# Four products a group moved behind the next group's eight, and one small load moved to another queue

## The chip, the cores and the metric

The kernel runs on one core of one Trainium2 chip. The metric is the device time of one execution in microseconds (us). Three executions of the kernel before took 1425.3, 1425.72 and 1429.72 us; the median is 1425.72 us.

## What is computed

One layer of a hybrid encoder on an input x of 256 rows by 2048 columns, in float32:

```python
h = rms_norm(x, norm_g)
u = h @ w_in                                    # 2048 x 22672
y_a, y_b, y_c, y_d = conv(u), rwkv7(u), forgetting_attention(u), pooling(u)   # 256 x 1024 each
merged = sum(sigmoid(logits_n(u) + b_merge[n]) * (y_n @ w_branch[n]) for n in range(4))
out = rms_norm(x + merged @ w_out, final_g)
```

Nearly all arithmetic is in three families of matrix products: with w_in (2048 x 22672), with the four w_branch (1024 x 2048) and with w_out (2048 x 2048). The weights are streamed from HBM once.

## The kernel before

**Chunks and groups.** A chunk is up to 512 columns of a weight matrix. It is computed for both 128-row blocks b = 0 and 1 of the 256 rows, each in its own PSUM bank (`psm`). The sum over the 2048 (or 1024) inputs goes in steps k of 128, and KG = 2 steps make a group g, so a chunk has 8 groups (4 for w_branch). There are 65 chunks: 45 of w_in, 16 of w_branch and 4 of w_out.

**Exact products from halves.** A float32 weight tile is split into a high part `wh` (a rounded copy) and a low part `wl` (the remainder); the activations are kept split in the same way (`xh` and `xl`, later `yah` and so on). Per step k and block b three products are added up in one bank: high activation by high weight (line 246), high activation by low weight (line 247), low activation by high weight (line 248). A group thus has 2 blocks x 2 steps x 3 = 12 products, each 128 x 128 by 128 x 512.

**The path of a group's weights.** SyncE (SP) loads a group's `raw` tile (line 265, 3 buffers). ScalarE (ACT) copies each of its two steps to `wh` (line 273; 6 buffers, that is three groups). VectorE (DVE) subtracts to get `wl` (line 274, 6 buffers). TensorE (PE) then runs the products. A `raw` buffer comes free when VectorE has made its `wl`; `wh` and `wl` buffers come free when the last product that reads them is done.

**Banks.** The pool of `psm` has three banks and a chunk takes two, in rotation. The first bank of a new chunk has long been empty; the second is the one that held block 0 of the chunk just ended, so the block 1 products of the new chunk wait until that one has been read out (by ScalarE at lines 290, 296, 304, 665 and so on, or by VectorE at lines 722, 734, 778, 860, 862, 899).

**Order.** Every engine has a list of instructions that it works off in order. A planner writes the lists ahead of time (line 951): of the instructions that are ready by its own timeline it takes the one with the best priority. Loads and splits of weights have the best priority (WEIGHTS), then the RWKV and attention chains, then everything else, the products among them, in the order of the program. ScalarE and VectorE also do all of the RWKV, attention, convolution and pooling work, mostly in the first 800 us; the products fill TensorE around it.

**The start.** `head(0)` loads the identity (line 173), then x_quarter(0) loads the first half quarter of x (line 207), the first step of the first weights (line 324), `norm_g` as `ng16` (line 326), the second half quarter and the second step, all on SP's queue. `norm_g` is transposed on TensorE (line 213), copied to `ngT` (line 214), and scales every `xh` and `xl` tile (lines 224, 225).

**The end.** The last w_out chunk (`keep`) computes block 0 group by group, keeping all split weights, and then block 1 from the kept ones.

Of the kernel before, what the change touches and what calls it, by code (L numbers as in the profile page):

```python
# [17 lines left out]
P = 128  # L18
T = 256
NB = 2  # L20
# [4 lines left out]
KG = 2  # L25
# [69 lines left out]
def kernel(  # L95
# [27 lines left out]
    nc = tc.nc  # L123
# [28 lines left out]
    @contextmanager  # L152
    def level(n):
        own, tc.cur_priority = tc.cur_priority, at[n]
        yield
        at[n], tc.cur_priority = tc.cur_priority, own
# [15 lines left out]
    def load_constants(lo, hi):  # L172
        nc.sync.dma_start(out=cst[:, lo:hi], in_=consts[:, lo:hi])
# [26 lines left out]
    ng16 = xin.tile([16, P], F32, name="ng16")  # L200

    def x_quarter(q):

        xt = xin.tile([P, NB, CH], F32, name=f"x{q}")
        for s in (range(2) if q == 0 else ()):
            cols = slice(s * CH // 2, (s + 1) * CH // 2)
            nc.sync.dma_start(out=xt[:, :, cols], in_=x_v[:, :, cols])
            first_weights(s)
        if q:
            nc.sync.dma_start(out=xt, in_=x_v[:, :, q * CH:(q + 1) * CH])  # L210
        if q == 0:
            tp = psum_ex("c")
            nc.tensor.transpose(tp[:, 0:16], ng16, ident[:16, :16])
            v.tensor_copy(out=ngT, in_=tp[:, 0:16])
        for k2 in range(2):
            tp = psum_ex("c" if k2 else "r")
            for j in range(2):
                for b in range(NB):
                    c0 = (2 * k2 + j) * P
                    nc.tensor.transpose(tp[:, j * T + b * P:j * T + (b + 1) * P], xt[:, b, c0:c0 + P], ident)  # L220
            for j in range(2):
                k = q * 4 + k2 * 2 + j
                s = tp[:, j * T:(j + 1) * T]
                last = sc.activation(out=xh[:, k, :], in_=s, func=AF.Copy, scale=ngT[:, k:k + 1])
                v.scalar_tensor_tensor(out=xl[:, k, :], in0=s, scalar=ngT[:, k:k + 1],
                                       in1=xh[:, k, :].bitcast(F32), op0=ALU.mult, op1=ALU.subtract)
        return xt, last
# [11 lines left out]
        v.tensor_scalar(out=nrstd8, in0=rstd, scalar1=-float(H) ** -0.5, scalar2=None, op0=ALU.mult)  # L239


    def products(ps, sth, stl, wh, wl, k, nk, n, b):
        cols = slice(b * P, (b + 1) * P)
        o = ps[b][:, :n]
        h, l = wh[:, :n], wl[:, :n]
        nc.tensor.matmul(o, lhsT=sth[:, k, cols], rhs=h, start=k == 0, stop=False)  # L246
        nc.tensor.matmul(o, lhsT=sth[:, k, cols], rhs=l, start=False, stop=False)  # L247
        nc.tensor.matmul(o, lhsT=stl[:, k, cols], rhs=h, start=False, stop=k == nk - 1)  # L248

    def new_ps():  # L250
        return [ps_main.tile([P, CH], F32, name="psm", tag="psm") for b in range(NB)]

    def chunk(ranges, nk, sth, stl, before=lambda g: None, keep=None):


        ps = new_ps()
        n = sum(r[2] for r in ranges)
        for g in range(nk // KG):
            wh, wl = [], []
            with level(WEIGHTS):  # L260
                raw = before(g)
                at = 0
                for wv, c0, w in ranges if raw is None else ():
                    raw = raw or wpool.tile([P, KG, CH], F32, name="raw", bufs=3)
                    nc.sync.dma_start(out=raw[:, :, at:at + w], in_=wv[:, g * KG:(g + 1) * KG, c0:c0 + w])
                    at += w
                for j in range(KG):
                    if keep:
                        h, l = keep(g * KG + j)
                    else:  # L270
                        h = wpool.tile([P, CH], F32R, name="wh", bufs=6)
                        l = wpool.tile([P, CH], F32R, name="wl", bufs=6)
                    sc.activation(out=h[:, :n], in_=raw[:, j, :n], func=AF.Copy)  # L273
                    v.tensor_tensor(out=l[:, :n], in0=raw[:, j, :n], in1=h[:, :n].bitcast(F32), op=ALU.subtract)  # L274
                    wh.append(h)
                    wl.append(l)
            for b in range(1 if keep else NB):
                for j in range(KG):
                    products(ps, sth, stl, wh[j], wl[j], g * KG + j, nk, n, b)
        if keep:  # L280
            for k in range(nk):
                products(ps, sth, stl, *keep(k), k, nk, n, 1)
        return ps

    def chunk_in(c0, n=CH, before=lambda g: None):
        return chunk([(w_in_v, c0, n)], D // P, xh, xl, before)
# [33 lines left out]
    def first_weights(j):  # L320

        if j == 0:
            first_raw.append(wpool.tile([P, KG, CH], F32, name="raw", bufs=3))
        nc.sync.dma_start(out=first_raw[0][:, j, :], in_=w_in_v[:, j, O_B + HALF:O_B + 2 * HALF])
        if j == 0:
            nc.sync.dma_start(out=ng16, in_=norm_g[0].rearrange("(k p) -> k p", p=P))

    def head(g):
        if g == 0:
            load_constants(0, P)  # L330
        if g == 6:
            load_constants(P, N_CONST)
        if g in (0, 1, 3, 5):
            xq.append(x_quarter(len(xq)))
        return first_raw[0] if g == 0 else None

    ps_first = chunk_in(O_B + HALF, before=head)
    with tc.issue_after(xq[3][1].ins):
        for q in range(4):
# [399 lines left out]
    def b_inputs(hf):  # L739
        t = [rw.tile([P, NB, HALF], F32, name="u" + nm) for nm in "rkv"]  # L740
        c0 = O_B + hf * HALF
        for j in range(3):
            if j == 2 and hf == 1:

                n0 = 328
                ps = chunk_in(c0 + 2 * W, n0)
                for b in range(NB):
                    sc.activation(out=t[2][:, b, 0:n0], in_=ps[b][:, 0:n0], func=AF.Copy, scale=rstd[:, b:b + 1])
                n1 = HALF - n0
                lu = wk.tile([P, NB, P], F32, name="qk", bufs=2)  # L750
                cf = wk.tile([P, NB, 16], F32, name="cf")
                ps = chunk([(w_in_v, c0 + 2 * W + n0, n1 + P), (w_in_v, O_CF, 16)], D // P, xh, xl)
                for b in range(NB):
                    for dst, lo, hi in ((t[2][:, b, n0:HALF], 0, n1), (lu[:, b, :], n1, n1 + P),
                                        (cf[:, b, :], n1 + P, n1 + P + 16)):
                        sc.activation(out=dst, in_=ps[b][:, lo:hi], func=AF.Copy, scale=rstd[:, b:b + 1])
                lora_and_forget(lu, cf)
            else:
                evac(t[j], ps_first if j == 0 and hf == 1 else chunk_in(c0 + j * W))
        return t  # L760
# [60 lines left out]
    for hf in range(2):  # L821
# [4 lines left out]
        for g2 in range(2):  # L826
            g = hf * 2 + g2
# [12 lines left out]
            for b in range(NB):  # L840
                for j in range(2):
                    nc.tensor.matmul(tp[:, b * T:(b + 1) * T], lhsT=pT[:, j, b * P:(b + 1) * P], rhs=pw[:, j, :],
                                     start=(j == 0), stop=(j == 1))
# [9 lines left out]
    for dc in range(4):  # L853
        mg = wk.tile([P, NB, CH], F32, name="va")
        for n, nm in enumerate("abcd"):
            gt = gate_tile(dc, n)
            ps = chunk([(w_br_v[n], dc * CH, CH)], W // P, *yT[nm])
            for b in range(NB):
                if n == 0:
                    v.tensor_tensor(out=mg[:, b, :], in0=ps[b], in1=gt[:, b, :], op=ALU.mult)  # L860
                else:
                    v.tensor_tensor(out=gt[:, b, :], in0=ps[b], in1=gt[:, b, :], op=ALU.mult)
                    v.tensor_tensor(out=mg[:, b, :], in0=mg[:, b, :], in1=gt[:, b, :], op=ALU.add)
        split_T([mh[dc // 2], ml[dc // 2]], (dc % 2) * 4, mg, 4)
# [18 lines left out]
    def keep(k):  # L883
        if k < 8:
            return spare[0][:, k, :], spare[1][:, k, :]
        i = 2 + 2 * ((k - 8) // 4)
        return spare[i][:, k % 4, :], spare[i + 1][:, k % 4, :]

    for dc in range(4):
        fg = bcast(final_g[dc * CH:(dc + 1) * CH])  # L890
        ps = chunk([(w_out_v, dc * CH, CH)], D // P, Parts(mh), Parts(ml), keep=keep if dc == 3 else None)
        cs = slice((dc % 2) * CH, (dc % 2 + 1) * CH)
        last = dc == 3
        n = CH // 2 if last else CH
# [60 lines left out]
```

## Time and profile before

| | |
|---|---|
| median of three executions | 1425.72 us |
| the profiled execution | 1430.22 us |
| its span, first to last instruction | 1428.4 us |
| PE busy | 1390.6 us (97%), 6961 matmuls and as many weight loads |
| DVE busy | 983.7 us (69%) |
| ACT busy | 743.1 us (52%) |
| HBM read | 257.44 MB |
| granted TensorE clock, mean | 0.995 |

Busy time of PE is modelled: matmuls overlap, and a row of one shows it longer than the distance to the next. So the distance from start to start tells the pace of TensorE, and its idle time, not its busy share, tells what can be won. The weight loads (PEld) run beside the matmuls. Of the 6961 matmuls 5472 are the products of the 65 chunks.

### The profile page before, as it was taken

What the parts mean: (1) busy time and instruction counts of PE and PEld (TensorE: products, weight loads), DVE (VectorE), ACT (ScalarE), POOL (GpSimd) and SP (SyncE); (2) the same over time, 40 slices, a digit from 0 to 9 for tenths busy, and PEclk for the clock granted to TensorE, in tenths of its full rate; (3) what the DMA queues carried; (4) which work ended last, traced back from release to release, by engine and by line L of the source; (5) the groups of instructions that cost most, each with busy time, mean ns of one, the idle gap of its engine ahead of it and who ended that gap; (6) DMA issues with size and microseconds to landing.
All of it is one profiled execution on the core that took longest, in us unless ns stands there. A gap on an engine that the chain in (4) does not pass through costs nothing.

```text
span 1428.4 us, 19730 instructions
## 1 busy us (share of the span) xinstructions
PE 1390.6 (97%) x6961; PEld 1150.9 (81%) x6961; DVE 983.7 (69%) x1724; ACT 743.1 (52%) x1298; POOL 75.4 (5%) x149
## 2 busy tenths in 40 slices
PE   8899999999999899999999999999999999999997
PEld 6787778887787687888788888888888888888885
DVE  5558879589766979769948656665665666566654
ACT  7455644554455465554535554455545545445454
POOL 0310000001002000010000000000000000000000
PEclk9999999999999999999999999999999999999999
DMA  7776546456557645546655566666666666776564
GB/s 254 201 218 199 172 140 182 135 143 204 163 152 215 194 147 177 164 135 187 183 166 158 159 199 200 203 197 201 203 197 200 200 201 199 224 236 202 190 207 146
DMA packets 136914, 266.17 MB, mean 186 GB/s; under 512 B 11609, under 2 KB 16392, under 8 KB 136816
## 3 DMA queue, kind: packets, MB, share of 16 engines
q1 hardware_dynamic: 128480, 239.83, 55.4%
q0 software_dynamic: 7760, 24.04, 6.5%
q8 instruction: 54, 0.88, 0.3%
q10 hardware_dynamic: 576, 1.05, 0.2%
q14 instruction: 44, 0.36, 0.1%
HBM read 257.44 MB, written 2.10 MB: 182 GB/s over the span
## 4 chain that ended last, share of the span: by engine, by line
PE 66%; DVE 13%; DMA 5%; issue 5%; ACT 1%; POOL 0%; DVEq 0%; ACTq 0%; POOLq 0%
PE psm L247 20%; PE psm L246 20%; PE psm L248 20%; DVE wl L274 4%; DVE MT L519 2%; DVE tm L526 2%; DMA raw<-in_w_in_dram 1%; DMA cg<-pz 1%; DVE UQ L528 1%; DMA raw<-in_w_out_dram 1%; PE ps_z L571 1%; PE ps_r L505 1%; PE ps_z L567 1%; PE ps_r L580 1%; DMA pv<-uv 1%
## 5 line engine op out<-in xcount | busy, mean ns | idle before, releaser
L273 ACT ACTIVATE wh<-raw 128x512 fp32r<-128x512 f32 (+1 forms) x896 | 544.9, 624 | 531.0 <-PE psm L248 346.4
L274 DVE TENSOR_TENSOR wl<-raw,wh 128x512 fp32r<-128x512 f32 (+1 forms) x896 | 596.3, 681 | 313.9 <-ACT wh L273 312.6
L247 PE MATMUL psm<-wl,xh 128*128 128x512 f32 (+1 forms) x1440 | 565.0, 394 | 12.9 <-DVE wl L274 12.7
L248 PE MATMUL psm<-wh,xl 128*128 128x512 f32 (+1 forms) x1440 | 560.8, 391 | 0.0
L246 PE MATMUL psm<-wh,xh 128*128 128x512 f32 (+1 forms) x1440 | 548.2, 393 | 4.7 <-ACT wh L273 2.9
L247 PEld LDWEIGHTS psm<-wl,xh 128*128 128x128 f32 x1440 | 272.0, 189 | 74.2 <-DVE wl L274 22.0
L246 PEld LDWEIGHTS psm<-wh,xh 128*128 128x128 f32 x1440 | 271.8, 189 | 62.0 <-ACT wh L273 4.9
L248 PEld LDWEIGHTS psm<-wh,xl 128*128 128x128 f32 x1440 | 271.9, 189 | 51.9 <-issue 0.5
L526 DVE TENSOR_TENSOR tm<-UQ,MT 128x16 f32<-128x16 f32 (+30 forms) x124 | 52.1, 420 | 2.0
L528 DVE TENSOR_REDUCE UQ<-tm 128x8 f32<-128x16 f32 (+30 forms) x124 | 36.1, 291 | 1.9
L184 POOL DMA_DIRECT2D row<-in_b_merge_dram x16 | 8.7, 542 | 503.8 <-DVE qa L778 435.0
L519 DVE STREAM_TRANSPOSE MT<-G 32x1024 f32<-32x1024 f32 x16 | 32.0, 1999 | 0.2
L778 DVE SCALAR_TENSOR_TENSOR qa<-psm,rstd,row 128x512 f32<-128x512 f32 x32 | 24.0, 751 | 9.5 <-PE psm L248 9.5
L695 ACT ACTIVATE pt<-pt,mx 128x128 f32<-128x128 f32 (+1 forms) x32 | 14.3, 449 | 24.7 <-DVE mx L693 24.6
L247 PE MATMUL psm<-wl,yah 128*128 128x512 f32 x64 | 24.9, 389 | 0.0
L248 PE MATMUL psm<-wh,yal 128*128 128x512 f32 x64 | 24.9, 389 | 0.0
L247 PE MATMUL psm<-wl,ybh 128*128 128x512 f32 x64 | 24.9, 389 | 0.0
L248 PE MATMUL psm<-wh,ybl 128*128 128x512 f32 x64 | 24.9, 389 | 0.0
L247 PE MATMUL psm<-wl,ych 128*128 128x512 f32 x64 | 24.9, 389 | 0.0
L248 PE MATMUL psm<-wh,ycl 128*128 128x512 f32 x64 | 24.9, 389 | 0.0
L247 PE MATMUL psm<-wl,ydh 128*128 128x512 f32 x64 | 24.9, 389 | 0.0
L248 PE MATMUL psm<-wh,ydl 128*128 128x512 f32 x64 | 24.9, 389 | 0.0
(381 smaller groups left out, 1390.3 us busy)
## 6 DMA issues: line engine op xcount, KB each, us to landing
raw<-in_w_in_dram SPq DMA_DIRECT2D x343, 512.0 KB, 4.3
raw<-in_w_branch_dram SPq DMA_DIRECT2D x64, 512.0 KB, 4.9
raw<-in_w_out_dram SPq DMA_DIRECT2D x32, 512.0 KB, 4.8
row<-in_b_merge_dram POOLq DMA_DIRECT2D x16, 256.0 KB, 4.4
raw<-in_w_in_dram SPq DMA_DIRECT2D x8, 328.0 KB, 4.4
raw<-in_w_in_dram SPq DMA_DIRECT2D x8, 312.0 KB, 3.5
cg<-pz POOLq DMA_DIRECT2D x4, 448.0 KB, 5.5
x<-in_x_dram SPq DMA_DIRECT2D x3, 512.0 KB, 8.1
```

The costliest lines, as they stand in the source:

```text
L246: nc.tensor.matmul(o, lhsT=sth[:, k, cols], rhs=h, start=k == 0, stop=False)
L247: nc.tensor.matmul(o, lhsT=sth[:, k, cols], rhs=l, start=False, stop=False)
L248: nc.tensor.matmul(o, lhsT=stl[:, k, cols], rhs=h, start=False, stop=k == nk - 1)
L273: sc.activation(out=h[:, :n], in_=raw[:, j, :n], func=AF.Copy)
L274: v.tensor_tensor(out=l[:, :n], in0=raw[:, j, :n], in1=h[:, :n].bitcast(F32), op=ALU.subtract)
L505: nc.tensor.matmul(gps[par][:, j * P:(j + 1) * P], lhsT=BK[:, i, par, e, :], rhs=GT[:, p2 + i, e, :], start=True, stop=True)
L519: v.transpose(out=MT[32 * q:32 * q + 32].rearrange("p t (r u) -> p t r u", u=NH), in_=src)
L526: v.tensor_tensor(out=tm[:, :, 0:n], in0=UQ[:, i:32, :].rearrange("p j c -> p c j"), in1=MT[:, i:32, i].unsqueeze(1).to_broadcast([P, 8, n ...
L528: v.tensor_reduce(out=UQ[:, i, :], in_=tm[:, :, 0:n], axis=AX.X, op=ALU.add)
L567: nc.tensor.matmul(o[0:MORE, p * P:(p + 1) * P], lhsT=after(GTt, 4 * p + 2 * e + part), rhs=SB[:, p, :], start=p == 0, stop=False)
L695: sc.activation(out=pt[:, s], in_=pt[:, s], func=AF.Exp, scale=-1.0, bias=mx[:, b:b + 1], accum_out=sm[:, b:b + 1])
L778: v.scalar_tensor_tensor(out=gt[:, b, :], in0=ps[b], scalar=rstd[:, b:b + 1], in1=bm, op0=ALU.mult, op1=ALU.add)
```

## The change

In each group the eight products with the high weights (both halves of the activations, lines 246 and 248 before) come first; the four with the low weights (line 247 before) are put off until the next group's eight are through. In a chunk's last group nothing is put off past its end: its eight, then the four of the group before, then its own four. The number of products, their operands and all loads and splits stay as they are. The `keep` chunk does the same for block 0, and for block 1 each step's two and then its one. And `norm_g` is loaded by ScalarE's queue, as the first thing of `head(0)`, and not by SP's queue behind the first weights.

```diff
-    def products(ps, sth, stl, wh, wl, k, nk, n, b):
-        cols = slice(b * P, (b + 1) * P)
-        o = ps[b][:, :n]
-        h, l = wh[:, :n], wl[:, :n]
-        nc.tensor.matmul(o, lhsT=sth[:, k, cols], rhs=h, start=k == 0, stop=False)
-        nc.tensor.matmul(o, lhsT=sth[:, k, cols], rhs=l, start=False, stop=False)
-        nc.tensor.matmul(o, lhsT=stl[:, k, cols], rhs=h, start=False, stop=k == nk - 1)
+    def with_high(ps, sth, stl, wh, k, n, b):
+
+        for st in (sth, stl):
+            nc.tensor.matmul(ps[b][:, :n], lhsT=st[:, k, b * P:(b + 1) * P], rhs=wh[:, :n],
+                             start=k == 0 and st is sth, stop=False)
+
+    def with_low(ps, sth, wl, k, nk, n, b):
+        nc.tensor.matmul(ps[b][:, :n], lhsT=sth[:, k, b * P:(b + 1) * P], rhs=wl[:, :n], start=False,
+                         stop=k == nk - 1)
...
+        late = []
         for g in range(nk // KG):
...
-            for b in range(1 if keep else NB):
+            bs = range(1 if keep else NB)
+            for b in bs:
                 for j in range(KG):
-                    products(ps, sth, stl, wh[j], wl[j], g * KG + j, nk, n, b)
+                    with_high(ps, sth, stl, wh[j], g * KG + j, n, b)
+
+            late.append((wl, g))
+            for wl, g in late[:] if g == nk // KG - 1 else late[:-1]:
+                for b in bs:
+                    for j in range(KG):
+                        with_low(ps, sth, wl[j], g * KG + j, nk, n, b)
+                late.pop(0)
         if keep:
             for k in range(nk):
-                products(ps, sth, stl, *keep(k), k, nk, n, 1)
+                with_high(ps, sth, stl, keep(k)[0], k, n, 1)
+                with_low(ps, sth, keep(k)[1], k, nk, n, 1)
...
         nc.sync.dma_start(out=first_raw[0][:, j, :], in_=w_in_v[:, j, O_B + HALF:O_B + 2 * HALF])
-        if j == 0:
-            nc.sync.dma_start(out=ng16, in_=norm_g[0].rearrange("(k p) -> k p", p=P))
 
     def head(g):
         if g == 0:
+            nc.scalar.dma_start(out=ng16, in_=norm_g[0].rearrange("(k p) -> k p", p=P))
             load_constants(0, P)
```

## Rows read from the trace of the kernel before

**Rows 1.** Windows of 100 us: busy time and instructions of each engine, granted clock, DMA share, GB/s.

```profile
0.00:100.00 100.00, 89.22 (x447) 77.01 (x448) 54.86 (x101) 57.99 (x123) 20.16 (x42) 0.98 0.77 220
...
400.00:500.00 100.00, 94.31 (x452) 75.07 (x451) 73.91 (x107) 51.65 (x84) 13.41 (x25) 1.00 0.66 190
...
800.00:900.00 100.00, 100.00 (x449) 82.76 (x448) 62.43 (x96) 52.48 (x81) 2.16 (x4) 1.00 0.65 196
```

**Rows 2.** Waits of PE, first 160 us: us in total, times, longest.

```profile
PE psm L247 <- DVE wl L274: 5.5, 5, 2.3
...
PE psm L246 <- ACT wh L273: 2.9, 4, 1.1
PE ps_c L213 <- DMA ng<-in_norm_g_dram: 1.5, 1, 1.5
```

**Rows 3.** Waits of PE from 160 to 800 us.

```profile
PE psm L247 <- DVE wl L274: 7.2, 9, 1.7
PE psm L246 <- DVE ya L305: 1.8, 2, 1.4
```

**Rows 4.** The page's costliest groups and DMA issues: the split and its load.

```profile
L273 ACT ACTIVATE wh<-raw 128x512 fp32r<-128x512 f32 (+1 forms) x896 | 544.9, 624 | 531.0 <-PE psm L248 346.4
L274 DVE TENSOR_TENSOR wl<-raw,wh 128x512 fp32r<-128x512 f32 (+1 forms) x896 | 596.3, 681 | 313.9 <-ACT wh L273 312.6
...
raw<-in_w_in_dram SPq DMA_DIRECT2D x343, 512.0 KB, 4.3
```

**Rows 5.** Waits of the whole span: ScalarE for the raw weights.

```profile
ACT wh L273 <- DMA raw<-in_w_in_dram: 120.8, 58, 6.7
```

**Rows 6.** Waits of SP's queue.

```profile
SPq L265 <- DVE wl L274: 1001.5, 386, 12.4
```

**Rows 7.** Timeline at the end of a chunk: start, us, engine, line, op.

```profile
1120.29 1.38 DVE L274 TENSOR_TENSOR wl<-raw,wh 128x512 fp32r<-128x512 f32 x2 [1.34 <-ACT wh L273]
...
1121.01 0.39 PE L247 MATMUL psm<-wl,xh 128*128 128x512 f32 x1
1121.24 0.39 PE L248 MATMUL psm<-wh,xl 128*128 128x512 f32 x1
...
1121.67 0.75 DVE L778 SCALAR_TENSOR_TENSOR qa<-psm,rstd,row 128x512 f32<-128x512 f32 x1
...
1122.83 0.39 PE L246 MATMUL psm<-wh,ybh 128*128 128x512 f32 x1
```

**Rows 8.** Timelines of DVE, ACT and PE around one wait.

```profile
190.10 6.01 DVE L519 STREAM_TRANSPOSE MT<-G 32x1024 f32<-32x1024 f32 x3
...
192.74 1.32 ACT L273 ACTIVATE wh<-raw 128x512 fp32r<-128x512 f32 x2 [0.15 <-PE psm L248]
...
194.84 0.39 PE L246 MATMUL psm<-wh,xh 128*128 128x512 f32 x1
196.89 0.50 PE L247 MATMUL psm<-wl,xh 128*128 128x512 f32 x1 [1.67 <-DVE wl L274]
```

**Rows 9.** Windows of 3.4 us with a low granted clock.

```profile
70.00:73.40 3.40, 2.87 (x10) 2.87 (x11) 3.40 (x7) 0.24 (x1) 0.58 (x1) 0.52 0.36 96
152.00:155.40 3.40, 3.25 (x8) 2.39 (x9) 3.40 (x6) 0.63 (x1) 0.00 (x0) 0.50 0.35 89
377.00:380.40 3.40, 2.52 (x6) 2.06 (x7) 3.30 (x6) 2.66 (x6) 0.00 (x0) 0.55 0.40 138
```

**Rows 10.** Timeline of the start.

```profile
2.16 0.43 SPq L326 DMA_DIRECT2D ng<-in_norm_g_dram  x1
2.63 0.42 SPq L207 DMA_DIRECT2D x<-in_x_dram  x1
...
6.65 0.63 ACT L273 ACTIVATE wh<-raw 128x512 fp32r<-128x512 f32 x1 [4.63 <-DMA raw<-in_w_in_dram]
7.04 0.18 PEld L213 LDWEIGHTS ps_c<-cst,ng 16*128 16x128 f32 x1 [1.90 <-DMA ng<-in_norm_g_dram]
...
8.35 1.20 PE L246 MATMUL psm<-wh,xh 128*128 128x512 f32 x2
```

## The prediction

> **What bounds the kernel now.** I read first the windows of 100 us, to see which engine is full where. From 800 to 1400 us TensorE is busy all the time: one such window stands there for six [rows 1]. Before 800 us it is not: 89% in the first window, 94% in the fifth [rows 1]. Next comes the pace, from the timeline at the end of a chunk: from 1121.24 to 1122.83 us seven products start, so one takes 0.227 us [rows 7]; its row shows 0.39 us. The low product at 1121.01, with another stationary tile than the one after it, has the same distance [rows 7]. So 5472 products are at most 1242 us of the 1428, and this sum doesn't change. The change can only win idle time of TensorE.
>
> The waits of PE say how much there is. It waits for `wl` 5.5 us in 5 waits before 160 us [rows 2], 7.2 us in 9 waits after [rows 3], and after 800 us its windows are full [rows 1]. A wait in this view begins where the modelled end of the last product is, 0.39 - 0.227 = 0.16 us late, so the true loss is 5.5 + 5 x 0.16 = 6.3 us and 7.2 + 9 x 0.16 = 8.6 us, together 14.9 us. For `wh` it waits 2.9 us in 4 waits, truly 3.5, all early [rows 2]; for a bank still being read 1.8 us [rows 3]. Three stretches of about 3.4 us show a granted clock of half, 1.2 instead of 2.4 GHz, each just behind such waits [rows 9]; at half pace each costs 1.7 us, together 5.1.
>
> **When a late VectorE costs time, before and after.** Count in products of 0.227 us, with group g of a chunk beginning at 12g. ScalarE's copy takes 0.62 us (2.7 products), VectorE's subtraction 0.68 (3), a load 4.3 us (19) [rows 4]. Say VectorE starts a group's two subtractions at s.
>
> Before, the first low product is due at 12g + 1, so s may be 12g - 2. VectorE's end, s + 6, also frees the `raw` buffer for group g + 3 (SP's queue waits mostly for this [rows 6]); its load and copy end at s + 27.7, and the high product is due at 12g + 36. That allows s up to 12g + 8.3, so the low product decides.
>
> After, a group's eight high products begin at 12g - 4 and its four low ones at 12g + 16. The low product allows s up to 12g + 13. But the high products of group g + 3 are due at 12g + 32, which allows s only up to 12g + 4.3. So VectorE may be 6.3 products, 1.4 us, later than now, not the 3.4 us by which the low product itself moves; then `raw` is late next. Buffers bind no earlier: `wl` of group g - 3 comes free at 12g - 16, eight products later than now, still 20 ahead of 12g + 4.3, and `wh` comes free eight earlier.
>
> One wait shows it. VectorE is in three transposes until 196.11 us, the subtraction follows, and TensorE, ready at 195.07, goes on at 196.89; the next group's `wh` was copied from 192.74 on [rows 8]. After the change its eight products fill this wait of 1.8 us, and the load that starts when the subtractions are done is what could then be late.
>
> **The sum.**
>
> *Low products, later part.* Nine waits, 8.6 us, 0.96 us in the mean, under 1.4; the longest, 1.7 + 0.16 [rows 3], keeps 0.5. I take 7.5 us off. Bounds: 0, if the planner puts other VectorE work into the new slack, and 8.6.
>
> *Low products, first 160 us.* 6.3 us, but here the loads are the late ones: DMA engines 77% busy [rows 1], and all the waits for `wh`. ScalarE's waits for `raw`, 120.8 us in 58 [rows 5], tell the same. What is won at a low product is there mostly paid at the next high one. I take a third, 2.1 us; bounds 0 and 6.3.
>
> *High products due four earlier.* 0.9 us more for each of the 4 waits for `wh`: at most +3.6 [rows 2], at least 0; three of four, +2.7.
>
> *Clock.* Of the three stretches at 1.2 GHz two (70 and 152 us [rows 9]) come where TensorE waits for `wl` and `wh` [rows 2], the third (377 us) where it waits for a bank [rows 3]. I take 2.3 off the 5.1; bounds 0 and 5.1.
>
> *norm_g.* SP issues it at 2.16 us, it lets TensorE go on at 7.04, and the first product follows at 8.35 [rows 10]. `wh` of that product was ready at 6.65 + 0.63 = 7.28, so an early `norm_g` can bring the first product to 7.3, 1.0 us earlier, no more. That it takes 4.9 us, though a load of 512 KB takes 4.3 [rows 4], says that it stands behind the x and weight loads on its queue. On SP each later load is issued 0.47 us earlier (2.63 - 2.16). On ScalarE nothing stands behind it, since its first copy waits for `raw` until 6.65 anyway [rows 10]. I take 0.8; bounds 0 and 1.0.
>
> The Trainium skill speaks against that cut ("DMA: Bandwidth & Descriptors", section "Issuing engines are not separate DMA queues"): DMAs of all engines interleave on the same 16 DMA engines, and another issuer saves only the sequencer's time for the issue. By that rule the term would be the 0.47 us of the issue and the whole sum 0.3 us smaller. The 4.9 us for so small a load lean the other way; no row here settles it.
>
> *Banks.* Block 0's last product before was the seventh from the chunk's end (1121.24 us); its read-out begins 0.43 us later, takes 0.75 and ends at 1122.42 [rows 7], 1.77 us before the new chunk's block 1 is due, six products past the boundary (1124.19). After, block 0 ends third from the end (read-out done 0.50 us past the boundary) and block 1 is due four products past it, at 0.91. That leaves 0.4 us. With the 64 boundaries bounded by 0 and, where a pair of subtractions of 1.38 us [rows 7] stands before the read-out, 64 x (1.38 - 0.41) = 62 us, I take +1.0: the nearest row leaves 0.4 us, and the planner can put block 0's next group in front.
>
> *Nothing.* Loads, copies and subtractions are the same in number; the last chunk needs no freed buffers, so its order costs nothing unless its loads are late.
>
> Sum: -7.5 - 2.1 + 2.7 - 2.3 - 0.8 + 1.0 = -9.0 us, 1430.2 to 1421.2 in the profiled execution. That execution is 4.5 us over the median, so on the median's scale 1425.7 - 9.0 = 1416.7 us.
>
> **Rivals.** Differences under 0.3%, 4.3 us, can hardly be measured here.
>
> *The wait moves to the high products* (0.24). Loads at 6 us and not 4.3 shift their arrival by 7.5 products, s goes to 12g - 3.2, and the 1.4 us are gone. For: ScalarE's 58 waits for `raw`, 2 us each in the mean [rows 5]. Against: only 4 of them reached TensorE, none after 160 us [rows 2]. Then some 3 of the 14.9 us are left, less norm_g's 0.8, plus the 2.7: -1 us, 1425.
>
> *All of it is won* (0.12): -14.9 - 5.1 - 1.0 = -21 us, 1404.7. It needs highs that are never late, against the calculation above.
>
> *The second bank is late: slower* (0.12). If at the boundaries a pair of subtractions goes ahead of the read-out, each loses up to 0.97 us. It decides from 0.14 us a boundary on (9.0 / 64), and gives slower by more than can be missed from 0.21 on; at 0.35 it is +22 - 9 = +13 us, 1439. For: late read-outs already cost 1.8 us in two waits [rows 3], with 1.4 us more room than after. Against: the planner sees the read-out in its own timeline and can hoist other products.
>
> The Trainium skill has this as a clock rule too ("TensorE: Matmul & The Clock Gate", section "A second HAM failure mode: psum-queue depth-cycling"): short idles of TensorE between bank turns make its clock swing. At 1.7 us for a stretch as in [rows 9], one at every fourth boundary would be 27 us. Here single waits of up to 1.8 us [rows 8] left the clock up, so it gets no more than 0.03 of the 0.12.
>
> *The planner undoes it* (0.05): it orders by readiness already, and the lists come out nearly as now, 1425.
>
> **Numbers.** The forecast, 0.47, covers -5 to -14 us: 1412 to 1421. 1416.7 is its middle. The range reaches to "all of it" at 1405 and past "no change" to 1428; outside lie the slower case and a little below, under 2 in 10. Faster: 0.47 + 0.12 and a little of the first rival, 0.60. Same: 0.28. Slower: 0.12.
>
> **What would show it.** Right: PE's waits for `wl` fall from 12.7 us to about 4, those for `wh` rise from 2.9 to 4 to 6, at most two stretches of low clock, the first product at about 7.5 us, and TensorE still full from 800 to 1400. Wrong: waits of PE for DVE or ACT at the first product of block 1 (bank), waits for `wh` over 8 us behind late loads, or a window after 800 us under 100.

## The result: slower by 1.1%, and the profile after

| | before | after |
|---|---|---|
| median of six executions | 1426.29 us | 1442.16 us (1434.75 to 1444.3) |
| ratio, 95% interval | | 1.0106 [1.0085, 1.0126] |
| span of the profiled execution | 1428.4 us | 1441.0 us |
| granted clock, mean | 0.995 | 0.990 |

The forecast was 1416.7 us, in a range of 1405 to 1428. The time lies outside, on the other side of no change.

In the kernel after, the high products are line 245, the low ones 249, ScalarE's copy 276, VectorE's subtraction 277, SP's load 268. First the windows; they answer to [rows 1].

```profile
0.00:100.00 100.00, 89.97 (x444) 76.95 (x445) 54.36 (x101) 56.11 (x122) 19.38 (x41) 0.98 0.77 220
...
800.00:900.00 100.00, 97.24 (x444) 80.53 (x443) 58.32 (x93) 46.63 (x80) 1.61 (x3) 1.00 0.61 185
900.00:1400.00 500.00, 500.00 (x2224) 414.35 (x2223) 292.55 (x459) 229.38 (x395) 10.07 (x18) 1.00 0.67 205
```

From 900 us on TensorE is as full as before, so all that was lost was lost in the first 900 us. Counting the 5472 products by their starts narrows it down: product 2800, at 808 us before, comes 12.6 us later after the change, and so does the last one. The waits of PE over the whole span answer to [rows 2, 3]:

```profile
PE psm L245 <- ACT wh L276: 12.6, 10, 2.7
PE psm L245 <- DVE yb L309: 3.8, 2, 2.5
...
PE psm L245 <- DVE yc L309: 2.8, 2, 1.6
PE psm L245 <- DVE pz L317: 2.8, 1, 2.8
...
PE psm L245 <- DVE ya L317: 1.7, 1, 1.7
...
PE psm L249 <- DVE wl L277: 0.3, 1, 0.3
```

The waits for `wl` are gone: 12.7 us in 14 have become 0.3 in one. But the waits for `wh` went from 2.9 to 12.6 us, and those for a bank that is still being read (`yb`, `yc`, `pz`, `ya`) from 1.8 to 11.1 us. The next view is the one to look at when a wait moves: the waits of the two engines that make the weights.

```profile
DVE wl L277 <- ACT wh L276: 138.2, 98, 4.9
DVE wl L277 <- PE psm L249: 100.1, 66, 3.3
...
ACT wh L276 <- DMA raw<-in_w_in_dram: 263.9, 139, 6.1
```

The second line is new: VectorE waits 66 times for a low product, which means for a `wl` buffer that TensorE has not yet read. Before there is no such line. And ScalarE's waits for `raw` have doubled, from 120.8 us in 58 [rows 5] to 263.9 in 139; in the first 800 us, where the time is lost, they grew by half, from 112.8 to 167.1 us. Loads take as long as before (4.3 us on the page of either kernel, [rows 4]); SP's queue waits for VectorE to free `raw` [rows 6], so they start later when VectorE is held up.

The stretch of [rows 8] shows how this reaches TensorE. These are timelines of DVE, ACT and PE after, around the same transposes.

```profile
192.88 0.69 DVE L277 TENSOR_TENSOR wl<-raw,wh 128x512 fp32r<-128x512 f32 x1
...
193.49 6.03 DVE L530 STREAM_TRANSPOSE MT<-G 32x1024 f32<-32x1024 f32 x3
200.28 2.00 DVE L530 STREAM_TRANSPOSE MT<-G 32x1024 f32<-32x1024 f32 x1
...
202.31 2.50 DVE L277 TENSOR_TENSOR wl<-raw,wh 128x512 fp32r<-128x512 f32 x4
...
203.93 1.15 ACT L276 ACTIVATE wh<-raw 128x512 fp32r<-128x512 f32 x2 [6.12 <-DMA raw<-in_w_in_dram]
207.43 1.15 ACT L276 ACTIVATE wh<-raw 128x512 fp32r<-128x512 f32 x2 [2.35 <-DMA raw<-in_w_in_dram]
...
208.12 0.69 PE L245 MATMUL psm<-wh,xh 128*128 128x512 f32 x1 [1.80 <-ACT wh L276]
```

Before, VectorE's eight microseconds of transposes cost a wait of 1.67 us for `wl`. Now TensorE gets past that place, but VectorE has freed almost no `raw`, ScalarE stands for 6.12 and 2.35 us without one, and the high products wait 1.80 us for its copy. What was won at the low products is paid eleven microseconds later, with more on top. ScalarE's long wait by itself isn't new. Before, behind the same transposes:

```profile
200.62 1.15 ACT L273 ACTIVATE wh<-raw 128x512 fp32r<-128x512 f32 x2 [6.56 <-DMA raw<-in_w_in_dram]
```

No product waited for a copy then. At 196.4 us four high parts lay ready in either kernel. When ScalarE had a `raw` tile again, at 200.62 us before and 203.93 after, two were left before and none after.

The banks tell another part of it. Timelines around the end of a chunk at 146.8 us:

```profile
148.20 1.27 ACT L308 ACTIVATE sg<-psm,rstd 128x512 f32<-128x512 f32 x2
...
149.62 1.28 DVE L277 TENSOR_TENSOR wl<-raw,wh 128x512 fp32r<-128x512 f32 x2
150.82 1.21 DVE L440 TENSOR_TENSOR a<-a,n 128x1024 f32<-128x1024 f32 x1
151.96 1.28 DVE L277 TENSOR_TENSOR wl<-raw,wh 128x512 fp32r<-128x512 f32 x2
153.16 1.40 DVE L309 SCALAR_TENSOR_TENSOR yb<-psm,rstd,sg 128x512 f32<-128x512 f32 x2
...
153.96 0.80 PE L245 MATMUL psm<-wh,xh 128*128 128x512 f32 x1 [2.50 <-DVE yb L309]
```

The sigmoid of this chunk is done at 149.47 us, and the read-out that frees the bank follows only at 153.16, behind four subtractions and another operation. TensorE had put block 0's products of the next groups ahead, ran out of them and waited 2.50 us. The other five waits aren't all of this kind. In two of them (1.34 and 1.19 us) VectorE itself stood waiting for the sigmoid, which ScalarE did late:

```profile
260.29 1.41 DVE L309 SCALAR_TENSOR_TENSOR yc<-psm,rstd,sg 128x512 f32<-128x512 f32 x2 [1.23 <-ACT sg L308]
```

Last the clock. Before, three stretches of 3.4 us show 1.2 GHz [rows 9]; after, there are seven (at 78.6, 153.7, 208.3, 351.6, 361.9, 467.7 and 699.8 us), among them one behind each of the two waits just shown. At 1.7 us each, as the prediction estimated, the four more cost 6.8 us.

```profile
153.70:157.10 3.40, 3.14 (x8) 2.48 (x9) 3.34 (x6) 1.44 (x3) 0.54 (x1) 0.51 0.58 171
208.30:211.70 3.40, 3.40 (x9) 2.54 (x9) 3.13 (x12) 1.44 (x3) 0.00 (x0) 0.50 0.67 196
```

Together: -12.4 (`wl`) + 9.7 (`wh`) + 9.3 (banks) + 6.8 (clock) = +13.4 us; the span grew by 12.6. This adds up rows of two profiled executions; it doesn't yet tell causes apart.

### The profile page after: what moved, and what is told of

The parts are those of the page before. It is cut to its first block, busy times and chain, and to the rows that moved or that the text cites. A ratio compares the mean times of both kernels' runs of the same rounds, so it can differ in the third digit from the quotient of the medians.

```text
span 1441.0 us, 20204 instructions
## 1 busy us (share of the span) xinstructions
PE 1395.0 (97%) x6961; PEld 1156.7 (80%) x6961; DVE 968.1 (67%) x1724; ACT 705.2 (49%) x1296; POOL 75.0 (5%) x149
## 4 chain that ended last, share of the span: by engine, by line
PE 80%; DVE 4%; DMA 4%; issue 2%; ACT 1%; POOL 0%; DVEq 0%; ACTq 0%; POOLq 0%
PE psm L245 48%; PE psm L249 24%; DMA raw<-in_w_in_dram 2%; DVE wl L277 2%; DMA raw<-in_w_out_dram 1%; PE ps_r L516 1%; PE ps_z L582 1%; DVE MT L530 1%; PE ps_z L578 1%; PE ps_r L591 1%; PE ps_c L853 0%; PE ps_r L506 0%; PE ps_c L693 0%; DMA cg<-pz 0%; PE ps_c L698 0%
## 5 line engine op out<-in xcount | busy, mean ns | idle before, releaser
L277 DVE TENSOR_TENSOR wl<-raw,wh 128x512 fp32r<-128x512 f32 (+1 forms) x896 | 574.9, 679 | 346.0 <-ACT wh L276 138.2
L276 ACT ACTIVATE wh<-raw 128x512 fp32r<-128x512 f32 (+1 forms) x896 | 508.5, 618 | 579.1 <-DMA raw<-in_w_in_dram 263.9
L245 PE MATMUL psm<-wh,xh 128*128 128x512 f32 (+1 forms) x1440 | 570.2, 397 | 24.1 <-ACT wh L276 12.6
L249 PE MATMUL psm<-wl,xh 128*128 128x512 f32 (+1 forms) x1440 | 401.0, 392 | 0.5 <-DVE wl L277 0.3
L249 PEld LDWEIGHTS psm<-wl,xh 128*128 128x128 f32 x1440 | 268.1, 189 | 56.0 <-DVE wl L277 2.9
L791 ACT ACTIVATE qa<-qa 128x1024 f32<-128x1024 f32 x16 | 17.0, 1061 | 34.3 <-DVE qa L789 34.3
L245 PE MATMUL psm<-wh,yah 128*128 128x512 f32 x64 | 24.9, 389 | 0.0
L245 PE MATMUL psm<-wh,ybh 128*128 128x512 f32 x64 | 24.9, 389 | 0.0
L245 PE MATMUL psm<-wh,ych 128*128 128x512 f32 x64 | 24.9, 389 | 0.0
L245 PE MATMUL psm<-wh,ydh 128*128 128x512 f32 x64 | 24.9, 389 | 0.0
```

The lines of the kernel that those rows point to most:

```text
L245: nc.tensor.matmul(ps[b][:, :n], lhsT=st[:, k, b * P:(b + 1) * P], rhs=wh[:, :n], start=k == 0 and st is sth, stop=False)
L249: nc.tensor.matmul(ps[b][:, :n], lhsT=sth[:, k, b * P:(b + 1) * P], rhs=wl[:, :n], start=False, stop=k == nk - 1)
L791: sc.activation(out=flat(gt), in_=flat(gt), func=AF.Sigmoid)
```

## The experiments

Diffs are against the changed kernel unless a line says otherwise, and ratios are to the kernel before. A theory had to say why `wh` and banks got late. **Held buffers**: every low pair stays unread eight products longer, so VectorE, with six low buffers, can't work as far ahead. **Late block 0**: in a chunk's last group block 0 now ends later, and its bank with it. **The order itself**: what the planner makes of late low products costs the time.

### Which part of the change: e1_norm_only, e2_order_only

The first is the kernel before with `norm_g` on ScalarE's queue; the second, whose edit is shown, is the changed kernel with the load back on SP's.

```diff
+        if j == 0:
+            nc.sync.dma_start(out=ng16, in_=norm_g[0].rearrange("(k p) -> k p", p=P))
...
-            nc.scalar.dma_start(out=ng16, in_=norm_g[0].rearrange("(k p) -> k p", p=P))
```

> The kernel before with norm_g on ScalarE's queue and nothing else. In the changed kernel norm_g reached TensorE at 2.84 us and not 7.04, but the first product started at 8.40 us and not 8.35, behind transposes that wait for the second half quarter of x. Theory 'no gain at the start': 0.0 us at the first product (8.3 to 8.5 us), time within 0.2% of before. Rival 'the prediction's term': first product near 7.5 us, 0.8 us off. Rival 'any new list costs some us': a difference of 4 us or more either way with the products unchanged.

> The kernel before with the new order of products and norm_g still on SP's queue. If the order carries the loss: +13 to +18 us (1439 to 1444), PE waits for wh 10 to 15 us, PE waits for read-outs at lines 309 and 317 (numbers of the changed kernel) some 10 us, for wl under 1. If norm_g's queue carries part of it: under +10 us.

Measured: norm_g alone 0.9998 [0.9985, 1.0012]; the order alone 1.0083 [1.0068, 1.0098], with 12.4 us of waits for `wh` and 110.6 us of VectorE waiting for low buffers. The order carries the loss, though e2's 1438.01 us lie 1 us under what was expected; whether the early `norm_g` adds to it (1442.16 us in the changed kernel) isn't told apart, since the two intervals overlap. Why the early `norm_g` gives nothing is seen at the start of the kernel after (compare [rows 10]):

```profile
0.74 0.42 ACTq L340 DMA_DIRECT2D ng<-in_norm_g_dram  x1
...
2.81 0.18 PEld L213 LDWEIGHTS ps_c<-cst,ng 16*128 16x128 f32 x1 [2.81 <-DMA ng<-in_norm_g_dram]
...
6.83 0.63 ACT L276 ACTIVATE wh<-raw 128x512 fp32r<-128x512 f32 x1 [4.36 <-DMA raw<-in_w_in_dram]
...
7.63 1.11 PE L220 MATMUL ps_c<-cst,x 128*128 128x128 f32 x4 [2.31 <-DMA x<-in_x_dram]
...
8.40 0.78 PE L245 MATMUL psm<-wh,xh 128*128 128x512 f32 x1
```

`norm_g` is there 4.2 us earlier, and `wh` is ready by 7.46. But on PE's list four transposes of the second part of x stand before the first product, and that part lands at 7.63. In e1 it landed later still, at 8.12, and the first product stood at 8.89 us, past the 8.3 to 8.5 that were expected.

### Late block 0: e3_last_group_by_block

The last group of each chunk is worked off block by block, block 0 with all its low products first, so that block 0 ends earlier.

```diff
+            last = g == nk // KG - 1
             for b in bs:
                 for j in range(KG):
                     with_high(ps, sth, stl, wh[j], g * KG + j, n, b)
+                if last:
+                    for wl0, g0 in late + [(wl, g)]:
+                        for j in range(KG):
+                            with_low(ps, sth, wl0[j], g0 * KG + j, nk, n, b)
...
```

> The changed kernel, but in a chunk's last group all that is left of block 0 (its four high, then four low products of both groups) goes before block 1, so that block 0's bank is done 8 products before the chunk's end instead of 2. Theory 'bank': the six waits for read-outs of the sigmoid chunks (11 us) fall to under 4 and the time falls by 7 to 11 us, to 1431 to 1435; the waits for wh (12.6 us) stay. Rival 'held low buffers': the waits for wh carry the loss, and the time stays within 3 us of the changed kernel's 1442.

Measured: 1.0098 [1.0083, 1.0112]. Most of the bank waits stay, 8.6 us against 11.1, so the late end of block 0 isn't what makes them, and the time didn't fall by the 7 to 11 us of the theory. The theory falls. The waits for `wh`, which should have stayed, went from 12.6 to 8.4 us.

### The low products in their own group: e4_lows_in_own_group

Each group's eight high products, then its own four low ones. A low product still comes up to seven products later than before the change, but its buffer is free at the group's end, as it was before.

```diff
-        late = []
...
-            late.append((wl, g))
-            for wl, g in late[:] if g == nk // KG - 1 else late[:-1]:
-                for b in bs:
-                    for j in range(KG):
-                        with_low(ps, sth, wl[j], g * KG + j, nk, n, b)
-                late.pop(0)
+            for b in bs:
+                for j in range(KG):
+                    with_low(ps, sth, wl[j], g * KG + j, nk, n, b)
```

> The changed kernel, but a group's four low products follow its own eight and not the next group's: no low buffer is held longer than before, and the low products are still due 7 products later than before. Block 0 ends two products before the chunk's end, as in the changed kernel. Theory 'held low buffers': waits for wh fall from 12.6 to under 5 us, VectorE's waits for PE (100 us) to near 0, time 1426 to 1434. Rival 'bank': time stays at 1438 to 1444, since the bank is as late as in the changed kernel.

Measured: 0.9964 [0.9952, 0.9976], faster than both kernels. Its waits of PE, DVE and ACT:

```profile
PE psm L249 <- DVE wl L276: 4.4, 6, 2.3
...
PE psm L245 <- ACT wh L275: 3.0, 4, 1.2
...
DVE wl L276 <- PE psm L249: 27.9, 22, 2.9
...
ACT wh L275 <- DMA raw<-in_w_in_dram: 155.1, 85, 6.9
```

Two thirds of the waits for `wl` of before are gone and those for `wh` are as they were. It went further than the theory said (1420.59 us against 1426 to 1434), while VectorE's waits for TensorE, 27.9 us, did not go to near 0. But this changes the order and the holding at once.

### Fewer low buffers in that order: e5_own_group_low5, e6_own_group_low4

Only the number of low buffers of e4 is changed, to five and to four; the edit shown is against e4.

```diff
-                        l = wpool.tile([P, CH], F32R, name="wl", bufs=6)
+                        l = wpool.tile([P, CH], F32R, name="wl", bufs=5)
```

> The kernel with a group's lows behind its own eight, but with 5 low buffers instead of 6, so that the buffer of a group's low tile comes free on average 18 products before the group begins instead of 24; in the changed kernel it is 16. Theory 'held low buffers': VectorE's waits for PE reach some 60 to 110 us and PE's waits for wh 6 to 13 us, and most of the loss comes back, 1430 to 1440. Rival 'it is the order itself' (lows behind the next group's highs): 1418 to 1424 as with 6.

> The same with 4 low buffers: free 12 products before the group begins, later than in the changed kernel. Theory 'held low buffers': at least the changed kernel's loss, 1440 or more. Rival 'it is the order itself': under 1426.

Measured: 1.0077 [1.0064, 1.0089] and 1.0101 [1.0086, 1.0116]. With the order of e4, one low buffer less costs over 1%. The lines of the run with five:

```profile
PE psm L249 <- DVE wl L276: 12.2, 15, 2.4
PE psm L245 <- ACT wh L275: 6.0, 5, 2.2
...
DVE wl L276 <- PE psm L249: 91.7, 90, 3.3
...
ACT wh L275 <- DMA raw<-in_w_in_dram: 271.3, 153, 7.4
```

VectorE's and ScalarE's lines look like those of the changed kernel. TensorE's do not: here it waits for `wl` as long as before the change, and for `wh` half as long as in the changed kernel. Too few low buffers cost the time in either order, but not at the same products.

### Block by block in the own group: e7_own_group_by_block, e8_own_group_last_by_block

In e7 each group does block 0's four high and two low products and then block 1's; in e8 only a chunk's last group does so.

```diff
             for b in bs:
                 for j in range(KG):
                     with_high(ps, sth, stl, wh[j], g * KG + j, n, b)
...
+                for j in range(KG):
+                    with_low(ps, sth, wl[j], g * KG + j, nk, n, b)
```

> In each group block 0's four high and two low products, then block 1's: the first low is due 4 products after the group's begin (before: 1, own group: 8), low buffers as before, block 0 ends 6 products before the chunk's end as before. By the deadline alone (VectorE may be 3 products later than before, 0.7 us, against 7 products) half of what the own-group order won: 1422 to 1424, PE's waits for wl 7 to 10 us. If the own-group order is slowed by the late end of block 0: better than it, 1416 to 1419.

> Lows behind the own group's eight, but the last group of a chunk block by block. If the late end of block 0 costs anything in the own-group order, 1416 to 1419; if not, 1419 to 1422 like it.

Measured: 0.998 [0.9967, 0.9994] and 0.9985 [0.9973, 0.9997]; neither is better than e4. e8's 1423.94 us lie above both of its expected ranges. Of e7 only the times are used. That block 0 ends later costs nothing that an earlier end wins back.

### More low buffers in the late order: e9_small_tiles_single, e10_late_lows_eight_low_buffers

This is the test from the other side: the order of the change is kept, and each pair gets the room that it is held for. To make room for the two (2 KB in each partition apiece), both runs keep small tiles of the chains once and not twice (`tm`, `qk`, `pt`, and `lu`, which shared the buffers of `qk`, in one of its own); e9 is that alone, e10 has eight low buffers besides.

```diff
-                        l = wpool.tile([P, CH], F32R, name="wl", bufs=6)
+                        l = wpool.tile([P, CH], F32R, name="wl", bufs=8)
...
-            tm = rw.tile([P, 8, 32], F32, name="tm", bufs=2)
+            tm = rw.tile([P, 8, 32], F32, name="tm", bufs=1)
...
-        qk = wk.tile([R, 2 * T], F32, name="qk", bufs=2)
+        qk = wk.tile([R, 2 * T], F32, name="qk", bufs=1)
...
-        pt = wk.tile([P, 3 * P], F32, name="pt", bufs=2)
+        pt = wk.tile([P, 3 * P], F32, name="pt", bufs=1)
...
-                lu = wk.tile([P, NB, P], F32, name="qk", bufs=2)
+                lu = wk.tile([P, NB, P], F32, name="lu")
```

> The changed kernel with four small tiles of the attention and RWKV chains kept once and not twice (two of them share no buffer any more), which frees 4 KB in each partition; still six low buffers. It is the base for the run with eight. Both theories: as the changed kernel, ratio 1.008 to 1.014, VectorE's wait for a low buffer (for the low products) 90 to 120 us.

> The same with eight low buffers: the low products stay a group late, as in the change, but the buffer of a group's pair is needed again only four groups later. Theory of the held low buffers: VectorE's wait for them falls from 100 us to under 30, ScalarE's for raw weights from 264 to under 180, TensorE's for wh from 12.6 to under 5, and for banks from 12 to under 5; ratio 0.993 to 1.000. Rival, that the late order itself costs the time (its bunch of low products at a chunk's end, or what the planner makes of it): still 1.005 to 1.014.

Measured: e9 1.0109 [1.008, 1.0137], as slow as the change; e10 0.9968 [0.9951, 0.9986]. Two buffers take the whole loss away, and more, so the late order by itself doesn't cost it. First e9's waits, then e10's:

```profile
PE psm L245 <- ACT wh L276: 11.9, 9, 2.6
...
DVE wl L277 <- PE psm L249: 114.9, 74, 3.0
...
ACT wh L276 <- DMA raw<-in_w_in_dram: 258.6, 138, 6.1
```

```profile
PE psm L245 <- ACT wh L276: 4.1, 4, 2.1
...
PE psm L245 <- DVE ya L317: 3.2, 2, 2.2
...
PE psm L245 <- DVE ya L745: 2.4, 2, 1.3
...
DVE wl L277 <- PE psm L249: 27.8, 21, 2.9
...
ACT wh L276 <- DMA raw<-in_w_in_dram: 132.2, 75, 6.1
```

PE has no line for `wl` at all in e10. Its bank waits are 8.0 us (with `yc` 1.7, `yb` 0.5 and `pz` 0.2, not shown) against 10.5 in e9, not the under 5 that was expected: the two buffers take away most of the waits for `wh` and little of those for banks. At the transposes shown above, e10 looks like this, VectorE first and then ScalarE:

```profile
188.61 8.11 DVE L530 STREAM_TRANSPOSE MT<-G 32x1024 f32<-32x1024 f32 x4
196.75 2.50 DVE L277 TENSOR_TENSOR wl<-raw,wh 128x512 fp32r<-128x512 f32 x4
199.25 1.28 DVE L277 TENSOR_TENSOR wl<-raw,wh 128x512 fp32r<-128x512 f32 x2
...
201.69 1.15 ACT L276 ACTIVATE wh<-raw 128x512 fp32r<-128x512 f32 x2 [3.87 <-PE psm L245]
```

All four transposes stand in one piece, six subtractions are caught up in a row behind them, and until 201.69 us ScalarE waits for TensorE, so it is ahead, where in the changed kernel it waited for `raw`. From 180 to 212 us no product waits.

### One buffer moved, and more than needed: e11_late_lows_five_high_seven_low, e12_own_group_eight_low_buffers

e11 is the changed kernel with five `wh` and seven `wl` buffers, the same memory; e12 is e4 with eight low buffers and the small tiles of e9.

```diff
-                        h = wpool.tile([P, CH], F32R, name="wh", bufs=6)
-                        l = wpool.tile([P, CH], F32R, name="wl", bufs=6)
+                        h = wpool.tile([P, CH], F32R, name="wh", bufs=5)
+                        l = wpool.tile([P, CH], F32R, name="wl", bufs=7)
```

> The changed kernel with one buffer moved from the high to the low parts, five wh and seven wl, in the same memory. Theory of the held low buffers: the seventh gives back about half of what the eighth would, and wh, which the change frees eight products sooner, can spare one: ratio 0.998 to 1.007, VectorE's wait for low buffers 30 to 70 us. Rival, that buffers don't matter in the late order: 1.008 to 1.014. If the high buffers bind as well: over 1.010 with ScalarE's waits for the high products far above 128 us.

> The low products in their own group behind its eight high ones, eight low buffers, small tiles kept once. If six were still short (VectorE waited 28 us in that order): 0.990 to 0.995. If the loads set the pace by then: 0.995 to 0.999, as with six (0.9964).

Measured: 1.0127 [1.0101, 1.0153] and 0.9976 [0.9959, 0.9993]. e11 missed what I expected first: the seventh buffer gave nothing back. Its lines:

```profile
DVE wl L277 <- PE psm L249: 106.9, 106, 3.7
...
ACT wh L276 <- PE psm L245: 220.9, 187, 4.6
```

VectorE's waits became shorter (1.0 us in the mean against 1.5) but not fewer, and ScalarE waits 220.9 us for a high buffer, against 127.8 us in 88 waits in the changed kernel. This is the sign that was written down for the third case, that the five high buffers bind. By itself it shows little, since ScalarE waits longer still for high buffers in faster kernels (346.4 us before [rows 4], 268.7 in e10). How much of the miss is due to them and how much to the odd numbers, where steps are taken in pairs, stays open. e12 is about as good as e4 and e10: beyond six, the own group has no use for buffers.

## Why the prediction was wrong

**The step that failed** is in the part on when a late VectorE costs time: "Buffers bind no earlier: `wl` of group g - 3 comes free at 12g - 16, eight products later than now, still 20 ahead of 12g + 4.3". It asks how late VectorE may be and takes any earlier start for free. But VectorE must at times be away for 8 us, nearly 36 products, and what carries TensorE over that is the stock made before. How large the stock can be hangs on how early VectorE may start, and the sentence itself says that this moved by eight products. The runs showed in its place that the low buffers do bind: eight instead of six of them, and nothing else, is the step from 1.0109 (e9) to 0.9968 (e10), and five instead of six in the own group the step from 0.9964 (e4) to 1.0077 (e5).

The prediction's own figures give an estimate of what the high parts lose. `wh` of group g + 3 is ready 27.7 products after VectorE starts group g. Before, the low buffers allowed this from 12g - 24 + 27.7 = 12g + 3.7 on. The six `wh` buffers allowed it only later: the first high part of group g is read until 12g + 9, and a copy takes 2.7, so 12g + 11.7. That these set the pace is seen in ScalarE's idle time before its copies, 346.4 of 531.0 us of which ended with a product's read [rows 4]. Due at 12g + 36, a copy could thus be at most 24 products early. After, `wh` comes free sooner, but the low buffers hold the copy back to 12g - 16 + 27.7 = 12g + 11.7, and it is due at 12g + 32: 20 products. The estimate is 4 products, 0.9 us, less for the high parts.

The traces hold it to the test. Matching each copy with the first product that reads it, by the names in the programs' instruction lists, gives the time for which a copy was ready and waiting. From 800 to 1400 us its median was 5.23 us before and 3.90 after, and one copy in ten had less than 3.88 and 1.66. From 160 to 800 us, where most of the time is lost, the medians are 5.70 and 4.55 us. Counting there the copies with under 0.5 us to spare:

| kernel | copies under 0.5 us | ratio |
|---|---|---|
| e4, own group, six low buffers | 2 | 0.9964 |
| e8, the same, last group by block | 2 | 0.9985 |
| e12, own group, eight | 3 | 0.9976 |
| e1, norm_g alone | 4 | 0.9998 |
| before | 5 | 1 |
| e10, late, eight | 8 | 0.9968 |
| e5, own group, five | 9 | 1.0077 |
| e6, own group, four | 13 | 1.0101 |
| e3, late, last group by block | 15 | 1.0098 |
| after; e2 | 19; 19 | 1.0106; 1.0083 |
| e9, late, small tiles once | 23 | 1.0109 |
| e11, late, five high, seven low | 23 | 1.0127 |

The count splits the fast kernels from the slow ones, though by a single copy (8 and 9 stand side by side), and it doesn't give the size. Low parts aren't in it: with under 0.5 us to spare there are 33 of them before, 6 after and none in e10. Nor does the median tell e10 from e9 (4.68 and 4.50 us from 160 to 800 us); what differs is the short end, where one copy in ten had under 2.06 and 1.39 us.

e10 against e9, and e5 against e4, change nothing about the products' order in the program, and each turns the result over. That it takes more low buffers to hold the parts longer, and that too few cost the time, is shown from both sides. What isn't shown is the path to each single wait. Most of VectorE's new direct waits, 86.6 of the 100.1 us, lie behind 800 us, where almost nothing is lost; in the first 800 us e9 and e10 have the same:

```profile
DVE wl L277 <- PE psm L249: 13.5, 13, 2.1
...
DVE wl L277 <- PE psm L249: 13.6, 8, 2.9
```

ScalarE's waits for `raw` in the first 800 us do fall from e9 to e10, from 158.8 to 93.5 us. So the two buffers work there by another way than the direct wait. Whether the planner fills the place of a subtraction that can't start with other VectorE work, as the orders around 150 us suggest, was only argued.

**The terms.** *Low products, later part and first 160 us*: taken at -9.6 us together, measured as good as all of it, 12.7 to 0.3. *High products due four earlier*: taken at +2.7, measured +9.7; that they are due earlier is the smaller part, since the order of e10 has the same due times and 4.1 us of waits. This is the term that the failed step left too small. *Clock*: taken at -2.3; it went up by about 6.8; the stretches came with the longer waits, and they vary (the profiled execution of e9, 1438.6 us, has four). *Banks*: taken at +1.0 for block 0's later end; measured +9.3. e3 shows that block 0's later end isn't the main cause (8.6 of the 11.1 us stay without it), and e10 against e9 that the low buffers aren't either (8.0 of 10.5 us stay); the cause of these waits is open. *norm_g*: taken at -0.8, measured 0; I had traced the first product back to `norm_g` and `wh`, and left out the transposes that stand before it in PE's list. *Nothing*: loads, copies and subtractions were indeed the same in number and length.

**The rivals.** "The wait moves to the high products" had the place and the mechanism of loads that come late; its error was to let no more come back than had been won. "The second bank is late: slower" had the sign and nearly the time (1439 for 1442.16), but the time was luck. At its 0.35 a boundary it needed 22 late read-outs; there were six, 11.1 us in all, and subtractions stood before some of them only. The rest of the loss came from `wh` and the clock. Of the signs that were written down against the forecast, three came true: waits for `wh` over 8 us behind late loads, waits of block 1 for a bank, and a window after 800 us under 100 (97.24).

**The two cited rules.** The load of `norm_g` was issued 1.42 us earlier (2.16 to 0.74) and used 4.2 us earlier, in at most 2.1 us instead of 4.9. The Trainium skill, "DMA: Bandwidth & Descriptors", section "Issuing engines are not separate DMA queues", allows another issuer only the sequencer's time for the issue. This case settles nothing on that, since the load also came first and not behind three others. The rule of the Trainium skill, "TensorE: Matmul & The Clock Gate", section "A second HAM failure mode: psum-queue depth-cycling", was priced in the prediction at a low stretch for every fourth boundary, sixteen. There are seven, and the two shown stand behind single waits of 1.80 and 2.50 us, one of them at a bank turn, not behind many short idles.

## What to carry to other kernels

To move a consumer later is to hold its buffer longer: before you count the slack that it wins for the producer, count by how much less the producer can work ahead, and set both against the longest time for which that producer is away. Here four products moved behind their own group's eight, with the buffers as they were, gave 0.9964, the best version found; a group further they cost 1.0106, and with two more buffers the further move gave no more than the near one (0.9968). When a wait vanishes from the bound engine's list, look at the waits of its producers: a new line "producer waits for consumer" there is a sign that the stock is short. It isn't a proof, since most of it lay here where nothing was lost; a run with more buffers and no other change is.

## What the runs showed of the hardware that was not expected

The first product stood at 8.35 us before and 8.40 after although `norm_g` was used 4.2 us earlier: the start was set by the second part of x, which landed at 7.63 us. And single waits of TensorE came with stretches of 3.4 us at 1.2 GHz. Each of the seven began within 2 us of the end of a wait of 1.70 to 3.35 us, among them the 1.80 us at 208.12. But not every such wait had one. [rows 8] had shown 1.67 us with the clock left up, and after the change a longer one left it up as well; the window around it shows 1.00:

```profile
820.67 0.50 PE L245 MATMUL psm<-wh,xh 128*128 128x512 f32 x1 [2.76 <-DVE pz L317]
...
815.00:830.00 15.00, 12.24 (x60) 9.99 (x60) 10.39 (x18) 6.88 (x13) 0.54 (x1) 1.00 0.50 156
```

What decides between them, no run here shows.
